# Splitting the S5 scan into four pieces and starting the next block's exchange ahead of a block's back rotation

## The chip, the cores and the metric

The kernel runs on one core of one Trainium2 chip. The core has five engines that run side by side, each through its own instructions strictly in order: TensorE (PE, matrix products and transposes), VectorE (DVE), ScalarE (ACT), GpSimd (POOL) and SyncE (SP, which here does nothing but issue DMA transfers). The metric is device microseconds (us) of one execution of the whole program.

## The reference, cut to what matters

A two-layer trunk over 1024 positions of 1024 channels. Layer 0 mixes positions with an S5 state-space mixer, layer 1 with a short gated convolution; each is followed by a SwiGLU feed-forward part and a gated per-layer embedding. The change touches the S5 mixer only:

```
def s5_mixer(u, ...):                 # u: 1024 positions x 64 groups x 16 channels
    bu = einsum('bcgk,gpk->bcgp', u, bb)      # drive of 64 complex states in each group
    h[t] = abar * h[t-1] + bu[t]              # complex diagonal recurrence over the positions
    y = real(einsum('bcgp,gkp->bcgk', h, c)) + d_skip * u
    val, gate = split(gelu(y) @ w_glu)        # the "glu" stage
    return val * sigmoid(gate)
```

## The kernel before

**Tiling.** The S5 mixer is done in eight blocks of eight groups. Positions are cut into 128 chunks of 8. Inside a chunk everything is matrix products; between the chunks a real recurrence is left, once the complex state of each chunk has been turned by a phase that makes its factor real. The 128 partitions hold the 64 real parts and the 64 imaginary parts of the states, so a complex rotation needs a copy of a tile with its two halves of 64 partitions swapped. Engines work on partitions in place, so the swap is done by two DMAs (`swapped`, L935), called the exchange here.

**A block's steps**, by the names in the code:
- `gen_in(b)` (L1127): ACT scales the input into `raw` slot r0, PE transposes it (L1138), ACT writes `U`; DVE makes two products `raw<-pwr,bbA` and `raw<-pwn,bbS` (slots r1, r2), PE adds and transposes them (L1151), ACT writes `wbt`.
- `states(b)` (L1199): PE multiplies `wbt` with `U` into the PSUM tile `pb` (L1202).
- `phases(l)` (L1106): DVE builds the phase table `ptab` of two blocks; `gen_phase(b)` (L1191) has POOL issue four DMAs that copy a block's part to `E`.
- `scan(b)` (L1205): DVE multiplies `pb` with the sines into `tmp` (two instructions, the turned part), the exchange brings `tmp` swapped to `tw`, DVE multiplies `pb` with the cosines into `sv` (the plain part), adds `tw`, runs eight scans into `gv` (L1221), and rotates back: two products into a `tmp` buffer, the P operand, and two in place in `gv`.
- `gen_out(b)` (L1155): DVE makes the output weights `W1` in three instructions, PE makes the kernel `kp` from them (L1170), ACT copies it out (L1172), POOL adds the skip term (L1176).
- `gen_swap(b)` (L1178): two DMAs write `W2`, the swapped `W1`. `gen_toeplitz(b, M)` (L1185): eight DMAs spread `kp` into the block Toeplitz matrix `M`.
- `outputs(b)` (L1229): PE, per group, `U` by `M`, P by `W1` and `gv` by `W2` (L1236 to L1238) into one PSUM bank per four groups; ACT applies GELU into `zt`.
- `channels(b, zt)` (L1243): PE transposes `zt` (L286), and the result is split in a high and a low part in `ulow` (L291 to L293), the operand of `glu`.

**Buffers.** `M`, `W2`, `sv`, `gv`, `kp`, `tw` and `zt` exist once; `W1`, `U`, `E`, `tmp` and `pb` twice. PE's short products share three PSUM banks (`tr`).

**Order.** The program text gives priorities, not the order itself: a list scheduler simulates the engines and, on each engine, issues the ready instruction that stands first in the text. The order it finds is then fixed, and every engine waits in order. `tc.issue_after(ins)` forces an instruction behind another on the same engine. Behind all the S5 work in priority stand the products of the embedding (`up_product`, L758, matmuls into `pstu`, six per tile, evacuated by ACT L770 and stored by SP L771): they fill PE's gaps, from a single PSUM bank. Their operands lie in `ulow`, whose columns `channels(4)` and later blocks overwrite, so they end before that.

**The loop** (L1258): `scan(b)`, then `gen_out(b+1)`, `outputs(b)`, `gen_phase(b+1)`, `states(b+1)`, `gen_swap(b+1)`, `gen_toeplitz(b+1)`, `gen_in(b+2)`, `channels(b)`. In the last round but one, `M` for block 7 takes a buffer of `E`, and `gen_swap(7)` comes last. After the loop `glu` loads `s5_w_glu` in pieces of 256 KB (L784), splits them into `uhigh`, whose memory belonged to the S5 tiles, and starts its products.

## Time and profile before

| | us |
|---|---|
| median of three runs | 2271.43 (2271.29 to 2271.55) |
| the profiled execution | 2275.46 |
| its span, first to last instruction | 2273.7 |
| around the span | 1.76 |
| first scan's sum starts (`sv<-sv,tw` of block 0) | 64.38 |
| last scan's sum starts (block 7) | 201.19 |
| `outputs(7)` starts | 208.21 |
| first product of `glu` | 220.45 |

Lines such as L1221 are those of the kernel before. A row of a timeline gives start, duration, engine, line, operation, written tile and read tiles, how many in one piece, and in brackets the idle time ahead of it with what ended that. SPq rows are the times that SP spent on issuing, not the transfers. A row of the table of waits gives the waiting instruction, what it waited for, the total in us, the number of times and the longest. Behind the S5 stage the diff changes only when the first weights of `glu` are asked for.

### The profile page before, as it was taken

Reading aid. Unit: us, or ns where it says so; the run is one execution under the profiler, and the core shown is the slowest. Engines: PE = TensorE matmul, PEld = TensorE weight load, DVE = VectorE, ACT = ScalarE, POOL = GpSimd, SP = SyncE. Lnnn points to the kernel's source line nnn. Section 1 sums busy time; section 2 is a strip of 40 time slices with the busy share of each in tenths; the row PEclk is TensorE's granted clock in tenths of the full one; section 3 lists DMA queues with packets and bytes.
Section 4 is the critical chain, followed back from the end, with each engine's and each line's share of the span. In section 5 each row is a group of like instructions: output and inputs, shape, how many; then the busy total and the mean of one; then the engine's idle time right before and its main releaser. Section 6 shows DMA issues by size and latency. Waiting matters only on the chain.

```text
span 2273.7 us, 27899 instructions
## 1 busy us (share of the span) xinstructions
PE 2172.8 (96%) x10001; PEld 1788.2 (79%) x10001; DVE 1646.1 (72%) x2746; ACT 910.4 (40%) x1731; POOL 359.7 (16%) x440
## 2 busy tenths in 40 slices
PE   6988999899999999999979999979999999899998
PEld 5776888688888877878868888868888888787887
DVE  7885325887777787887587776397777777788864
ACT  6554323444444443334343332154444444333342
POOL 2110001011111112342010000111111111224210
PEclk9999999899999999999989999999999999999999
DMA  7555201254444468664232334623444445876713
GB/s 247 155 130 144 91 19 60 86 169 148 158 148 157 148 227 305 249 237 166 98 107 84 93 93 146 243 93 121 160 146 157 148 156 166 330 264 222 251 64 111
DMA packets 234011, 358.14 MB, mean 158 GB/s; under 512 B 23697, under 2 KB 166033, under 8 KB 233873
## 3 DMA queue, kind: packets, MB, share of 16 engines
q1 hardware_dynamic: 203040, 247.24, 33.5%
q0 software_dynamic: 30432, 109.08, 13.6%
q8 instruction: 79, 1.29, 0.2%
q14 instruction: 60, 0.48, 0.1%
q10 hardware_dynamic: 400, 0.04, 0.0%
HBM read 225.53 MB, written 114.29 MB: 149 GB/s over the span
## 4 chain that ended last, share of the span: by engine, by line
PE 62%; issue 18%; DVE 10%; DMA 5%; POOL 3%; ACT 1%; SPq 1%; POOLq 0%; DVEq 0%; ACTq 0%
PE psmm L124 20%; PE psmm L126 20%; PE psmm L125 20%; POOL hw L485 2%; DMA w<-hw 2%; DMA tw<-tmp 1%; DVE ulow L91 1%; DVE h L627 1%; DVE gv L1221 1%; DVE W L871 1%; DVE tmp L871 1%; DVE uhigh L91 1%; PE pstr L204 1%; DVE raw L871 0%; DVE ptab L871 0%
## 5 line engine op out<-in xcount | busy, mean ns | idle before, releaser
L124 PE MATMUL psmm<-ulow,ws 128*128 128x512 f32 x896 | 354.1, 396 | 14.9 <-ACT ulow L90 9.2
L126 PE MATMUL psmm<-ulow,ws 128*128 128x512 f32 x896 | 353.0, 394 | 4.7 <-DVE ws L91 4.7
L125 PE MATMUL psmm<-ulow,ws 128*128 128x512 f32 x896 | 353.5, 395 | 0.4 <-DVE ulow L91 0.4
L126 PE MATMUL psmm<-uhigh,ws 128*128 128x512 f32 x672 | 261.6, 389 | 0.0
L125 PE MATMUL psmm<-uhigh,ws 128*128 128x512 f32 x672 | 261.5, 389 | 0.0
L124 PE MATMUL psmm<-uhigh,ws 128*128 128x512 f32 x672 | 261.5, 389 | 0.0
L90 ACT CAST ws<-raw 128x512 fp32r<-128x512 f32 x224 | 138.9, 622 | 253.7 <-PE psmm L126 248.8
L485 POOL DMA_DIRECT2D hw<-hs x154 | 116.0, 754 | 772.7 <-DVE hs L91 746.6
L124 PEld LDWEIGHTS psmm<-ulow,ws 128*128 128x128 f32 x896 | 170.9, 191 | 52.9 <-ACT ulow L90 10.8
L126 PEld LDWEIGHTS psmm<-ulow,ws 128*128 128x128 f32 x896 | 170.7, 191 | 42.4 <-DVE ws L91 6.8
L125 PEld LDWEIGHTS psmm<-ulow,ws 128*128 128x128 f32 x896 | 170.8, 191 | 37.0 <-DVE ulow L91 1.5
L627 DVE TENSOR_TENSOR h<-psmm,h 128x512 f32<-128x512 f32 x234 | 155.3, 682 | 47.9 <-PE psmm L126 29.5
L636 POOL TENSOR_TENSOR h<-part,h 128x512 f32<-128x512 f32 x100 | 139.2, 1396 | 269.9 <-ACT part L635 239.4
L124 PE MATMUL psmm<-ulow,w 128*128 128x512 f32 x380 | 152.3, 401 | 17.0 <-DVE h L627 13.4
L91 DVE TENSOR_TENSOR ws<-raw,ws 128x512 fp32r<-128x512 f32 x224 | 153.7, 688 | 13.0 <-ACT ws L90 12.9
L90 ACT CAST ws<-st 128x512 fp32r<-128x512 f32 x168 | 103.8, 619 | 130.8 <-PE psmm L126 118.9
L125 PE MATMUL psmm<-ulow,w 128*128 128x512 f32 x380 | 149.4, 393 | 0.0
L126 PE MATMUL psmm<-ulow,w 128*128 128x512 f32 x380 | 149.3, 393 | 0.0
L125 PEld LDWEIGHTS psmm<-uhigh,ws 128*128 128x128 f32 x672 | 126.2, 188 | 26.2
L124 PEld LDWEIGHTS psmm<-uhigh,ws 128*128 128x128 f32 x672 | 126.2, 188 | 26.1
L126 PEld LDWEIGHTS psmm<-uhigh,ws 128*128 128x128 f32 x672 | 126.2, 188 | 26.1
L124 PE MATMUL psmm<-w,ulow 128*128 128x512 f32 (+1 forms) x360 | 139.1, 386 | 0.0
(263 smaller groups left out, 4433.7 us busy)
## 6 DMA issues: line engine op xcount, KB each, us to landing
hw<-hs POOLq DMA_DIRECT2D x154, 512.0 KB, 4.2
w<-hw SPq DMA_DIRECT2D x88, 768.0 KB, 6.0
raw<-in_ffn_w_in_dram SPq DMA_DIRECT2D x88, 512.0 KB, 3.9
raw<-in_ffn_w_out_dram SPq DMA_DIRECT2D x44, 512.0 KB, 6.1
hd<-h POOLq DMA_DIRECT2D x24, 512.0 KB, 3.0
h<-hd SPq DMA_DIRECT2D x24, 512.0 KB, 7.3
raw<-in_conv_w_in_dram SPq DMA_DIRECT2D x24, 512.0 KB, 3.8
w<-hw SPq DMA_DIRECT2D x88, 128.0 KB, 6.1
```

Of the source, the lines that this page charges most:

```text
L90: A.copy(hi, src)
L91: V.tensor_tensor(lo, src, hi.bitcast(F32), ALU.subtract)
L124: PE.matmul(ps, ahi, bhi, start=start, stop=False, skip_group_check=more)
L125: PE.matmul(ps, ahi, blo, start=False, stop=False, skip_group_check=more)
L126: PE.matmul(ps, alo, bhi, start=False, stop=stop, skip_group_check=more)
L204: PE.transpose(pt[:, c * P:(c + 1) * P], xn[:, c * P:(c + 1) * P], ident)
L485: nc.gpsimd.dma_start(out=hidden[j][:, :, c].rearrange("q p l j -> p q l j"), in_=hs.bitcast(F32))
L627: done["sum"] = V.tensor_tensor(h[t][:, cs], ps, h[t][:, cs], ALU.add).ins
L636: G.tensor_tensor(h[t][:, cs], part, h[t][:, cs], ALU.add)
L871: V.tensor_tensor(o, a, b, op)
L1221: V.tensor_tensor_scan(gv[:, g, 1:P], dec, sv[:, g, 1:P], 0.0, ALU.mult, ALU.add)
```

## The change

`scan` is cut in four: `scan_turned` (turned part and exchange), `scan_plain`, `scan_run` (sum and scans) and `scan_back`. Round b now runs `gen_out(b+1)`, `scan_run(b)`, `scan_turned(b+1)`, `scan_back(b)`, `scan_plain(b+1)`, `outputs(b)`, `gen_toeplitz(b+1)`, `gen_swap(b+1)`, `phases`, `gen_phase(b+2)`, `gen_in(b+2)`, `states(b+2)`, `channels(b)`. `states` and `gen_phase` stand a block earlier than before. The two products of `gen_in` are forced behind the latest `scan_plain`. Block 7 gets `M` and `W2` in two halves of four groups each, in the columns of `ulow` that `channels(7)` will fill: its `gen_swap` is four DMAs, its `gen_toeplitz` sixteen, and both are issued in round 6 ahead of `scan_back(6)`. The loads of three of the four weight pieces of `glu`'s first stage are issued in round 5.

```diff
+    def glu_load(nb, u):
+        wg = s5_w_glu[0].rearrange("(kt p) (two n) -> p kt two n", p=P, two=2)
+        raw = raw_tile()
+        rv = raw.rearrange("p (kt two n) -> p kt two n", kt=2, two=2)
+        for k in range(2):
+            nc.sync.dma_start(out=rv[:, k], in_=wg[:, 2 * u + k, :, nb * 256:(nb + 1) * 256])
+        return raw
...
-                raw = raw_tile()
...
+                raw = glu_raws.pop(0) if glu_raws else glu_load(nb, u)
...
@@ -1142,7 +1148,8 @@
         shp = [P, GB, T, KG]
         Wp = [raw_tile(i).rearrange("p (g t k) -> p g t k", g=GB, t=T) for i in (1, 2)]
         for o, pw, bb in ((Wp[0], pwr, bbA), (Wp[1], pwn, bbS)):
-            tt(o, pw[:, gsl, 0:T].unsqueeze(3).broadcast_to(shp), bb[:, gsl].unsqueeze(2).broadcast_to(shp), ALU.mult)
+            with tc.issue_after(done["plain"]) if b > 1 else ExitStack():
+                tt(o, pw[:, gsl, 0:T].unsqueeze(3).broadcast_to(shp), bb[:, gsl].unsqueeze(2).broadcast_to(shp), ALU.mult)
         wbt = wbts[b] = gen.tile([P, GB, P], F32, name="wbt", tag="wbt")
         for hf in range(2):
             pt = psum(tr)
@@ -1175,18 +1182,30 @@
                         dk[:, gsl].unsqueeze(2).broadcast_to([KG, GB, KG]), ALU.mult)
         G.tensor_tensor(kp[:, :, 0, :], kp[:, :, 0, :], dd, ALU.add)
 
-    def gen_swap(b):
+    def halves(a):
+        return [a[:, hf * 4:hf * 4 + 4] for hf in range(2)]
+
+    def late_halves(q):
+        return [ulow[:, q + hf, (KT - 1) * 4 * P:KT * 4 * P].bitcast(F32).rearrange("p (g n) -> p g n", g=4) for hf in range(2)]
+
+    def gen_swap(b, parts=None):
         W1 = Ws[b]
-        W2 = W2s[b] = run.tile([P, GB, T, KG], F32, name="W2", tag="W2")
-        for a, c in ((R0, R1), (R1, R0)):
-            nc.sync.dma_start(out=W2[a].rearrange("p g s k -> p g (s k)"),
-                              in_=W1[c, :, 1:NL, :].rearrange("p g s k -> p g (s k)"))
-
-    def gen_toeplitz(b, M):
-        Ms[b], kp = M, kps[b]
-        Mv = M.rearrange("p g (t k) -> p g t k", t=T)
-        for s in range(T):
-            nc.sync.dma_start(out=Mv[s * KG:(s + 1) * KG, :, T - 1 - s:, :], in_=kp[:, :, 0:s + 1, :])
+        if parts is None:
+            parts = [run.tile([P, GB, P], F32, name="W2", tag="W2")]
+        n = GB // len(parts)
+        for i, W2 in enumerate(parts):
+            for a, c in ((R0, R1), (R1, R0)):
+                nc.sync.dma_start(out=W2[a], in_=W1[c, i * n:(i + 1) * n, 1:NL, :].rearrange("p g s k -> p g (s k)"))
+        W2s[b] = parts if len(parts) == 2 else halves(parts[0])
+
+    def gen_toeplitz(b, parts):
+        kp = kps[b]
+        n = GB // len(parts)
+        for i, part in enumerate(parts):
+            Mv = part.rearrange("p g (t k) -> p g t k", t=T)
+            for s in range(T):
+                nc.sync.dma_start(out=Mv[s * KG:(s + 1) * KG, :, T - 1 - s:, :], in_=kp[:, i * n:(i + 1) * n, 0:s + 1, :])
+        Ms[b] = parts if len(parts) == 2 else halves(parts[0])
 
     def gen_phase(b):
         E = Es[b] = run.tile([P, 2, GB, NJ], F32, name="E", tag="E", bufs=2)
@@ -1202,28 +1221,35 @@
             PE.matmul(pb[:, g * P:(g + 1) * P], wbts[b][:, g, :], Us[b][:, g, :], start=True, stop=True)
         Bs[b] = pb.rearrange("p (g j) -> p g j", g=GB)
 
-    def scan(b):
-        B = Bs[b]
-        C, S_ = Es[b][:, 0], Es[b][:, 1]
-        parts = ((slice(0, NJ - 1), slice(1, NJ), slice(NJ - 1, 0, -1), sgnN, sgnA),
-                 (slice(NJ - 1, P - 1), slice(NJ, P), slice(0, NJ), sgnA, sgnN))
+    PARTS = ((slice(0, NJ - 1), slice(1, NJ), slice(NJ - 1, 0, -1), sgnN, sgnA),
+             (slice(NJ - 1, P - 1), slice(NJ, P), slice(0, NJ), sgnA, sgnN))
+    tws = {}
+
+    def scan_turned(b):
         tm = tmp_tile()[:, 0:GB * (P - 1)]
         tv = tm.rearrange("p (g j) -> p g j", g=GB)
-        for j, _, m, _, sg in parts:
-            stt(tv[:, :, j], B[:, :, j], sg, S_[:, :, m], ALU.mult, ALU.mult)
-        tw = gen.tile([P, GB * (P - 1)], F32, name="tw", tag="tw")
-        swapped(tw, tm)
-        for j, w, m, _, _ in parts:
-            tt(sv[:, :, w], B[:, :, j], C[:, :, m], ALU.mult)
-        tt(sv[:, :, 1:P], sv[:, :, 1:P], tw.rearrange("p (g j) -> p g j", g=GB), ALU.add)
+        for j, _, m, _, sg in PARTS:
+            stt(tv[:, :, j], Bs[b][:, :, j], sg, Es[b][:, 1][:, :, m], ALU.mult, ALU.mult)
+        tws[b] = gen.tile([P, GB * (P - 1)], F32, name="tw", tag="tw")
+        swapped(tws[b], tm)
+
+    def scan_plain(b):
+        for j, w, m, _, _ in PARTS:
+            done["plain"] = V.tensor_tensor(sv[:, :, w], Bs[b][:, :, j], Es[b][:, 0][:, :, m], ALU.mult).ins
+
+    def scan_run(b):
+        tt(sv[:, :, 1:P], sv[:, :, 1:P], tws[b].rearrange("p (g j) -> p g j", g=GB), ALU.add)
         for g in range(GB):
             dec = r8[:, b * GB + g:b * GB + g + 1].broadcast_to([P, P - 1])
             V.tensor_tensor_scan(gv[:, g, 1:P], dec, sv[:, g, 1:P], 0.0, ALU.mult, ALU.add)
+
+    def scan_back(b):
+        C, S_ = Es[b][:, 0], Es[b][:, 1]
         pv = Ps[b] = tmp_tile().rearrange("p (g j) -> p g j", g=GB)
         G.memset(pv[:, :, 0:1], 0.0)
-        for _, w, m, sg, _ in parts:
+        for _, w, m, sg, _ in PARTS:
             tt(pv[:, :, w], gv[:, :, w], C[:, :, m], ALU.mult)
-        for _, w, m, sg, _ in parts:
+        for _, w, m, sg, _ in PARTS:
             stt(gv[:, :, w], gv[:, :, w], sg, S_[:, :, m], ALU.mult, ALU.mult)
 
     def outputs(b):
@@ -1233,9 +1259,9 @@
             for c in range(4):
                 g = 4 * hf + c
                 o = py[:, c * P:(c + 1) * P]
-                PE.matmul(o, Us[b][:, g, :], Ms[b][:, g, :], start=True, stop=False)
+                PE.matmul(o, Us[b][:, g, :], Ms[b][hf][:, c, :], start=True, stop=False)
                 PE.matmul(o, Ps[b][:, g, :], Ws[b][:, g, 1:NL, :], start=False, stop=False)
-                PE.matmul(o, gv[:, g, :], W2s[b][:, g], start=False, stop=True)
+                PE.matmul(o, gv[:, g, :], W2s[b][hf][:, c, :], start=False, stop=True)
             A.activation(zt[:, :, hf * 64:hf * 64 + 64].rearrange("p t (g k) -> p g t k", k=KG),
                          py.rearrange("p (g t k) -> p g t k", g=4, t=T), AF.Gelu_apprx_tanh)
         return zt
@@ -1251,37 +1277,44 @@
     phases(0)
     states(0)
     gen_phase(0)
+    scan_turned(0)
+    scan_plain(0)
     gen_out(0)
     gen_swap(0)
-    gen_toeplitz(0, M)
+    gen_toeplitz(0, [M])
     gen_in(1)
+    states(1)
+    gen_phase(1)
     for b in range(NBT):
-        scan(b)
-        nx = b + 1
+        nx, after = b + 1, b + 2
+        if nx < NBT:
+            gen_out(nx)
+        scan_run(b)
+        if nx < NBT:
+            scan_turned(nx)
+            if nx == NBT - 1:
+                late = late_halves(0)
+                for part in late:
+                    G.memset(part, 0.0)
+                gen_swap(nx, late_halves(2))
+                gen_toeplitz(nx, late)
+        scan_back(b)
+        if nx < NBT:
+            scan_plain(nx)
+        zt = outputs(b)
         if nx < NBT - 1:
-            if b % LB == 0 and b // LB + 1 < NBT // LB:
-                phases(b // LB + 1)
-            gen_out(nx)
-            zt = outputs(b)
-            gen_phase(nx)
-            states(nx)
+            gen_toeplitz(nx, [M])
             gen_swap(nx)
-            gen_toeplitz(nx, M)
-            if b + 2 < NBT:
-                gen_in(b + 2)
+        if after < NBT:
+            if after % LB == 0:
+                phases(after // LB)
+            gen_phase(after)
+            gen_in(after)
+            states(after)
+            if after == NBT - 1:
+                glu_raws.extend(glu_load(0, u) for u in range(3))
+        if nx < NBT:
             channels(b, zt)
-        elif nx < NBT:
-            states(nx)
-            gen_phase(nx)
-            gen_out(nx)
-            M = run.tile([P, GB, P], F32, name="M", tag="E", bufs=2)
-            G.memset(M, 0.0)
-            gen_toeplitz(nx, M)
-            zt = outputs(b)
-            channels(b, zt)
-            gen_swap(nx)
-        else:
-            zt = outputs(b)
     gen.release()
     mb.release()
     tu.release()
```

More of the change, by code (lines that the diff above doesn't have):

```diff
@@ L771, in up_product @@
                     nc.sync.dma_start(out=updram[l][:, t, cs], in_=ev)
+    glu_raws = []
+    def glu_load(nb, u):
[5 more added lines that the diff above has]
+        return raw
     def glu(post, ahead):
-        wg = s5_w_glu[0].rearrange("(kt p) (two n) -> p kt two n", p=P, two=2)
         rooms = [[room_high(i) for i in range(4)], [room_new(i) for i in range(4)],
@@ L780, in glu @@
             for u in range(KT // 2):
-                raw = raw_tile()
-                rv = raw.rearrange("p (kt two n) -> p kt two n", kt=2, two=2)
-                for k in range(2):
-                    nc.sync.dma_start(out=rv[:, k], in_=wg[:, 2 * u + k, :, cs])
+                raw = glu_raws.pop(0) if glu_raws else glu_load(nb, u)
                 units.append([a.rearrange("p (kt n) -> p kt n", kt=2) for a in unit_of(rooms[nb][u](), raw)])
```

## Prediction

> **What bounds the kernel now.** I read the page first, then the timeline around the S5 mixer, then the waits and the stretches inside it.
>
> ```profile
> span 2273.7 us, 27899 instructions
> ...
> PE   6988999899999999999979999979999999899998
> ...
> DVE  7885325887777787887587776397777777788864
> ```
>
> A slice is 56.8 us. PE is at 8 or 9 tenths almost everywhere, so only what shortens PE's idle stretches can win time. The change sits in slices 1 to 3, where DVE too is at 8 tenths. Its stretches, cut where the output products of blocks 0 and 5 end, and its waits:
>
> ```profile
> core 0: us, PE busy (x) PEld busy (x) DVE busy (x) ACT busy (x) POOL busy (x), PEclk, DMA share, GB/s
> 55.00:81.30 26.30, 22.98 (x157) 19.29 (x156) 20.77 (x48) 13.67 (x32) 2.23 (x6) 1.00 0.58 164
> 81.30:183.70 102.40, 93.79 (x670) 81.62 (x669) 84.58 (x166) 58.79 (x153) 19.55 (x38) 0.98 0.58 141
> ```
>
> ```profile
> DVE sv L871 <- DMA tw<-tmp: 11.3, 4, 4.6
> DVE tmp L875 <- DMA E<-ptab: 1.0, 1, 1.0
> PE pstu L124 <- ACT ev L770: 4.4, 4, 1.1
> PE pstr L1170 <- DVE W L871: 3.6, 3, 2.6
> PE pstr L286 <- ACT wbt L1153: 0.6, 1, 0.6
> ```
>
> The waits are those of 81.3 to 183.7, five rounds of 20.5 us. DVE waits there 12.3 us (11.3 + 1.0), nearly all for the exchange. PE waits 8.6 us, which is also all that its 102.4 us have beside 93.79 busy. Two engines near full, and the smaller reserve is PE's. Over the whole stage, 55 to 221, with its start and end, DVE's wait for the exchange is:
>
> ```profile
> DVE sv L871 <- DMA tw<-tmp: 23.7, 8, 5.4
> ```
>
> **What removes the exchange wait.** One block on DVE and its exchange:
>
> ```profile
> 176.84 0.75 DVE L875 SCALAR_TENSOR_TENSOR tmp<-pb,sgnN,E 128x512 f32<-128x512 f32 x1
> 177.51 1.27 DVE L871 TENSOR_TENSOR sv<-pb,E 128x504 f32<-128x504 f32 x2
> 184.14 1.22 DVE L871 TENSOR_TENSOR sv<-sv,tw 128x1016 f32<-128x1016 f32 x1 [5.36 <-DMA tw<-tmp]
> ...
> 191.37 1.28 DVE L871 TENSOR_TENSOR tmp<-gv,E 128x504 f32<-128x504 f32 x2
> 192.57 0.73 DVE L875 SCALAR_TENSOR_TENSOR gv<-gv,sgnN,E 128x504 f32<-128x504 f32 x1
> 193.22 0.74 DVE L875 SCALAR_TENSOR_TENSOR gv<-gv,sgnA,E 128x512 f32<-128x512 f32 x1
> ```
>
> The turned part ends at 177.6, the sum starts at 184.1: 6.5 us, of which the plain part covers 1.3. The change puts the back rotation (1.28 + 0.73 + 0.74 = 2.75) and the plain part behind the exchange's start, 4.0 us, and the products of the input (two, of the size of the sum, 2.4) behind those: 6.4 us against 6.5. The exchange is covered, as far as DVE goes.
>
> **What is late next.** Three rings remain, and I price each.
>
> The first is M and W2, which exist once. After the products of block 5, SP refills them:
>
> ```profile
> 183.30 0.67 SPq L1189 DMA_DIRECT2D M<-kp  x1
> 184.06 1.31 SPq L1182 DMA_DIRECT2D W<-W  x2
> 185.42 5.38 SPq L1189 DMA_DIRECT2D M<-kp  x7
> ```
>
> ```profile
> 183.29 0.39 PE L1238 MATMUL pstr<-W,gv 128*128 128x128 f32 x2
> ...
> 194.71 0.49 PE L1236 MATMUL pstr<-M,U 128*128 128x128 f32 x2
> ...
> 199.73 0.39 PE L1237 MATMUL pstr<-W,tmp 128*128 128x128 f32 x2
> 199.95 0.39 PE L1238 MATMUL pstr<-W,gv 128*128 128x128 f32 x2
> ...
> 220.45 0.74 PE L124 MATMUL psmm<-uhigh,ulow 128*128 128x512 f32 x2 [0.60 <-ACT uhigh L90]
> ```
>
> Ten issues take until 190.8, the data some 3 us more, and block 6's products run from 194.7 to 200.3. From end to end 16.7 us: no round can be shorter, but the mean round (20.5) has 3.8 us above it, 19 in five rounds. The change swaps the order (M first, then W2) at the same count, so this floor stays. SP also issues the exchange (two issues) and the stores of the embedding; an exchange asked for just after a block's products queues behind these ten issues, up to 7.5 us. It is then needed only a round later (16.7 us, of which 7.5 + 6.5 are used), so I cost that at nothing; if the cover is gone each further microsecond costs one per round.
>
> The second is DVE's own work: its waits, 12.3 us, are the most that it can give back in these rounds. E's load (POOL) moves a block ahead and stands behind the phase table; it has the scans and weights of a round to cover it, and its 1.0 us goes with the rest.
>
> The third is PE: 8.6 us of idle in the five rounds, and no matmul is removed. The embedding's products do not vanish with the gaps that they filled. Of the idle time, 3.6 is PE waiting for W. Today those three instructions come behind the sum on DVE, so they inherit the exchange wait; after the change they stand ahead of it. I take 3.6 as gone. The 4.4 are pairs of embedding tiles one behind the other, with one PSUM bank between them, which happens when PE has nothing else; with a fuller PE I take a little over half, 2.4, as gone. Together **6.0 us** in the five rounds, between 0 (every gap comes back elsewhere) and 8.6.
>
> On the first stretch, 55 to 81.3: the first exchange can't be covered by a back rotation, as there is none. DVE loses the two products of the input as cover (they are now forced behind the plain part) and gets block 1's weights and the phase table instead. PE has 3.3 us idle there. I take **1.0**, between -1 and 3.3.
>
> **The end.** From the end of block 5's products (183.7) to that of block 7's:
>
> ```profile
> 195.53 0.45 POOL L1176 TENSOR_TENSOR kp<-kp,dd 16x128 f32<-16x128 f32 x1 [0.55 <-DMA raw<-in_s_w_glu_dram]
> ```
>
> ```profile
> 197.51 6.08 SPq L1189 DMA_DIRECT2D M<-kp  x8
> 203.69 1.33 SPq L1182 DMA_DIRECT2D W<-W  x2
> ```
>
> ```profile
> 208.21 0.77 PE L1236 MATMUL pstr<-M,U 128*128 128x128 f32 x2 [4.87 <-DMA W<-W]
> ...
> 216.44 0.39 PE L1238 MATMUL pstr<-W,gv 128*128 128x128 f32 x2
> ```
>
> Before: 33.1 us (216.8 - 183.7). PE waits for W2, which SP issues last, after eight issues for M at 0.76 each, since both W2 and M's queue place wait for block 6. With rooms of its own W2 goes early. But kp exists once: block 7's kp is done 12.3 us after block 5's products (196.0 - 183.7), because block 6's M must have been read out of it first, and this doesn't change. Then sixteen issues instead of eight. No row shows a half-size one; the nearest are M's own eight, whose landing hardly goes with their size:
>
> ```profile
> M<-kp SPq DMA_DIRECT2D x8, 64.0 KB, 3.0
> ...
> M<-kp SPq DMA_DIRECT2D x8, 8.0 KB, 3.0
> ```
>
> So I price them as full ones: 16 x 0.76 = 12.2, at most, and 6.1 if half a transfer costs half. The last lands at 12.3 + 12.2 + 3.0 = 27.5, and the second half of the products (half of 5.6, by block 6) ends at 30.3, the first half being done by then. That gains 2.8; block 7's products ran at half speed at first (0.77 for a pair against 0.39) and took 8.6 instead of 5.6, so a slow second half costs 1.5 and leaves 1.3. I take **2.0**, between 1.3 and 8 (2.8 with the six-us price of the issues and a full clock). The early loads of glu:
>
> ```profile
> 191.24 1.92 SPq L784 DMA_DIRECT2D raw<-in_s_w_glu_dram  x3
> ```
>
> Six of them (0.64 each) are asked for in round 5, some of which SP made later before; they stand ahead of kp's 12.3 us and cost nothing unless M's issues slip behind them, then 3.8 at most. Behind the products nothing changes: 3.6 us to glu's first product, and from there PE is gapless, so what S5 gains reaches the end.
>
> On the slow clock: PE had 4.9 us without work ahead of 208.2, and its pairs then took twice as long. The same followed a shorter gap:
>
> ```profile
> 131.28 1.07 PE L1170 MATMUL pstr<-W,bbA 128*16 128x128 f32 x8 [2.62 <-DVE W L871]
> 132.28 0.80 PE L292 MATMUL pstr<-ulow,identn 128*128 128x512 f32 x1
> ```
>
> A single L292 there took 0.80. The gap ahead of the last products will be near 3 us, so I keep them slow. The Trainium skill (TensorE: Matmul & The Clock Gate, Part 1) has the clock halved after an idle window of about 3.4 us; by that rule the last products would run at full speed and the sum would be 1.5 us better. The 2.62 us gap with slow products behind it speaks against relying on it.
>
> **Sum.** 1.0 + 6.0 + 2.0 = 9.0 us. Profiled execution: 2275.46 - 9.0 = 2266.5; the median before is 4.03 under that execution, so **2262.4** for the median. A difference of 0.2% (4.5 us) is about what a measurement of this kernel tells from none.
>
> **Rivals.**
>
> *PE has more room than its busy time says.* Then DVE's 12.3 us come back in full, with 3.3 at the start and 2 to 3 at the end: 17 to 18 us, 2254. For: PEld is busy only 81.62 of 102.4. Against: in the stretches where the timeline shows PE back to back, pairs start every 0.22 us (199.73, 199.95) and nothing fits between them. The Trainium skill (Perfetto Trace Analysis, Identifying the Most-Contended Engine) says that matmul busy time is a bad measure of PE's headroom and that weight-load busy time is a good one, which is this rival. Chance 0.13.
>
> *The gaps move.* The waits of PE and DVE reappear at other places: DVE at the sum for an exchange that queued behind SP's refill, PE at W or ev, or the scheduler puts the turned part behind the back rotation after all, because `pb` isn't ready, so that the order hardly changes. Then 0 to 4 us remain: 2269. Against: DVE has 6.4 us of work to set behind the exchange. Chance 0.20.
>
> *Slower: DVE stands at the turned part.* It comes ahead of the back rotation now and needs the states of the next block, whose input buffer U is free only after the products of the block two before. After block 3's products (143.2) the states' second half was done late, after block 5's soon:
>
> ```profile
> 142.97 0.39 PE L1238 MATMUL pstr<-W,gv 128*128 128x128 f32 x2
> ...
> 153.14 1.05 PE L1202 MATMUL pb<-U,wbt 128*128 128x128 f32 x8
> ```
>
> ```profile
> 187.40 1.95 PE L1202 MATMUL pb<-U,wbt 128*128 128x128 f32 x16
> ```
>
> That is 11.0 and 5.7 us (189.35 - 183.68). If DVE waits in order until 11.0, a round is 11.0 + 1.5 (turned) + 2.75 (back) + 6.7 (from the back rotation's end to that of the products, 193.96 to 200.3, and some queueing) = 21.9 against 20.5: 1.4 in each of five rounds, 7 us, less 2 at the end: 2276. It decides from 9.6 us on. For: all of ACT's work on the input lies in this path. Against: a scheduler that sees pb late will run the back rotation first. Chance 0.14.
>
> **How the numbers follow.** The forecast (6 to 12 us gained) has 0.53. Faster by over 0.2%: 0.53 + 0.13 and a little of the gaps' case, 0.68; within: 0.18; slower 0.14. The forecast's own range is 2259 to 2266. The range for eight in ten reaches to the middle of the first rival (2255) and to the end of the second (2271.5).
>
> **What would show it.** Right: the wait of the sum for the exchange falls from 23.7 us in all to under 5; the five rounds between the ends of the products of blocks 0 and 5 take 96 us instead of 102.4, with PE busy 93 to 94 in them; PE's wait for W is gone; the last products wait for M, not for W2, and glu starts near 211.5. Wrong: rounds of 17 to 18 us (first rival), rounds of 20 with new waits at ev, W or the exchange (second), DVE waiting for PE L1202 (third). A stage behind S5 that gets longer or shorter by over 2 us would be wrong for all four.

## The result

The changed kernel is slower. It takes 1.0078 of the time of the kernel before (95% interval 1.0064 to 1.0092). Three runs of it, 2286.07 to 2292.24 us, are used; two others, at far lower granted clocks (0.75 and 0.30), are left out. The profiled execution went from 2275.46 to 2289.14 us, its span from 2273.7 to 2287.0. The forecast was 2262.4, so it missed by about 27 us and had the wrong sign.

All of it lies in S5. The next stage's first product starts at 234.65 us instead of 220.45, which is 14.2 later, and what follows takes as long as before to 1 us (2052.4 against 2053.3 to the end of the span). The stretches of the changed kernel, cut as before at the ends of the output products of blocks 0 and 5 and at that first product:

```profile
55.00:86.10 31.10, 27.85 (x175) 22.00 (x174) 29.18 (x63) 15.01 (x35) 6.21 (x9) 1.00 0.62 169
86.10:197.70 111.60, 95.92 (x663) 82.97 (x662) 88.22 (x164) 58.57 (x151) 21.47 (x37) 0.95 0.49 120
197.70:234.70 37.00, 26.97 (x179) 22.65 (x177) 14.21 (x25) 13.19 (x29) 1.26 (x4) 0.86 0.52 129
```

The start is 4.8 us longer (26.3 before), the five rounds 9.1 (102.4 before), the end 0.2 (36.8 before, 183.7 to 220.45). Where DVE and PE wait between 55 and 235:

```profile
DVE tmp L881 <- issue: 14.3, 3, 6.0
...
PE pstr L1264 <- DVE gv L881: 10.9, 6, 4.0
...
DVE sv L877 <- DMA tw<-tmp: 9.7, 2, 8.6
...
DVE tmp L881 <- PE pb L1221: 5.9, 1, 5.9
PE pb L1221 <- ACT wbt L1160: 5.8, 5, 2.1
...
PE pstr L1262 <- DMA ulow<-kp: 5.6, 1, 5.6
```

The wait of the sum (`sv`) for the exchange has fallen from 23.7 us in eight to 9.7 in two, and both of these lie outside the five rounds. Inside them it is gone. In its place DVE waits at the first instruction of the turned part (`tmp L881`), and PE waits for the last instruction of the back rotation (`gv L881`). One round of the changed kernel on DVE, after block 0's products ended at 86.11:

```profile
94.62 0.74 DVE L881 SCALAR_TENSOR_TENSOR tmp<-pb,sgnA,E 128x504 f32<-128x504 f32 x1 [5.92 <-PE pb L1221]
95.28 1.27 DVE L877 TENSOR_TENSOR tmp<-gv,E 128x504 f32<-128x504 f32 x2
96.48 0.74 DVE L881 SCALAR_TENSOR_TENSOR tmp<-pb,sgnN,E 128x512 f32<-128x512 f32 x1
97.14 1.27 DVE L1238 TENSOR_TENSOR sv<-pb,E 128x504 f32<-128x504 f32 x2
98.32 1.22 DVE L877 TENSOR_TENSOR raw<-pwr,bbA 128x1024 f32<-128x1024 f32 x1
99.46 1.49 DVE L877 TENSOR_TENSOR raw<-pwn,bbS 128x1024 f32<-128x1024 f32 x1
100.87 0.88 DVE L881 SCALAR_TENSOR_TENSOR gv<-gv,sgnN,E 128x504 f32<-128x504 f32 x1
101.67 0.74 DVE L881 SCALAR_TENSOR_TENSOR gv<-gv,sgnA,E 128x512 f32<-128x512 f32 x1
```

Read it as a chain. The products of block 0 free U, and `pb` of block 2 is ready 8.5 us later. Only then does DVE start the turned part, and the back rotation of block 1 (`tmp<-gv`, then the two `gv<-gv`) stands behind it, although its scans were long done. Between the two halves of the back rotation stand the plain part (1.27) and the two products of the input (2.6). It ends at 102.4, the products of block 1 at 107.4: a round of 21.3 us. In the second and fourth round the phase table runs in the wait, and a round takes 23.7, but not because of the table: the back rotation ends 16.6 and 16.2 us after the products, as in the first round (16.3). The rest is PE's. In the second round it takes the first product of `gv` 2.4 us after `gv` is ready (126.44 against 124.04), behind products of the embedding; in the fourth the products run slowly.

PE loses twice. Two of its waits for `gv` are long, and the products behind them run slowly. From the timeline of PE, and the stretches of the fourth and fifth round:

```profile
168.44 0.79 PE L1264 MATMUL pstr<-W,gv 128*128 128x128 f32 x2 [4.00 <-DVE gv L881]
...
169.45 0.63 PE L1263 MATMUL pstr<-W,tmp 128*128 128x128 f32 x2
```

```profile
152.16:175.82 23.66, 17.21 (x116) 15.14 (x115) 21.18 (x50) 10.01 (x28) 3.37 (x7) 0.86 0.36 80
175.82:197.65 21.83, 15.93 (x116) 13.86 (x115) 15.43 (x23) 9.90 (x28) 4.22 (x7) 0.92 0.39 87
```

A pair takes 0.63 instead of 0.39 us, and the granted clock is 0.86 and 0.92 there.

### The profile page after: what moved, and what is told of

Its sections match the earlier page's. It is cut to its first block, busy times and chain, and to the rows that moved or that the text cites. A ratio compares the mean times of both kernels' runs of the same rounds, so it can differ in the third digit from the quotient of the medians.

```text
span 2287.0 us, 27932 instructions
## 1 busy us (share of the span) xinstructions
PE 2181.0 (95%) x10001; PEld 1792.1 (78%) x10001; DVE 1650.6 (72%) x2746; ACT 910.8 (40%) x1731; POOL 365.2 (16%) x441
## 4 chain that ended last, share of the span: by engine, by line
PE 51%; issue 31%; DVE 6%; DMA 5%; POOL 4%; SPq 1%; ACT 1%; POOLq 0%; DVEq 0%; ACTq 0%
PE psmm L124 15%; PE psmm L125 15%; PE psmm L126 15%; POOL hw L485 4%; DMA w<-hw 1%; DMA tw<-tmp 1%; DVE ulow L91 1%; DVE h L627 1%; DMA hw<-hs 1%; PE pstr L1264 1%; PE pstr L204 1%; PE pstr L1262 0%; DVE ws L91 0%; PE pstr L1263 0%; DVE uhigh L91 0%
## 5 line engine op out<-in xcount | busy, mean ns | idle before, releaser
L124 PE MATMUL psmm<-ulow,ws 128*128 128x512 f32 x896 | 354.2, 396 | 15.7 <-ACT ulow L90 10.1
L124 PEld LDWEIGHTS psmm<-ulow,ws 128*128 128x128 f32 x896 | 170.9, 191 | 53.3 <-ACT ulow L90 11.6
L124 PE MATMUL psmm<-ulow,w 128*128 128x512 f32 x380 | 152.2, 401 | 15.1 <-DVE h L627 12.9
```

Of the source, the lines that this page charges most:

```text
L124: PE.matmul(ps, ahi, bhi, start=start, stop=False, skip_group_check=more)
```

## The experiments

Times are medians. Each run stood beside runs of the kernel before on its own chip (2271.0 to 2273.9), and the ratio is to those. The stretches are read from the profiles, cut as above: "start ends" is the end of block 0's output products, "five rounds" go from there to the end of block 5's, and "end" from there to the first product of `glu`. "Gate" stands for the `issue_after` that forces the two products of `gen_in` behind the plain part.

| run | us | ratio (95%) | start ends | five rounds | end |
|---|---|---|---|---|---|
| before | - | 1 | 81.3 | 102.4 | 36.8 |
| changed | 2289.1 | 1.0078 (1.0064-1.0092) | 86.1 | 111.5 | 37.0 |
| e1 back first | 2269.6 | 0.9980 (0.9970-0.9990) | 79.7 | 101.1 | 36.9 |
| e2 own buffer | 2270.8 | 0.9990 (0.9981-1.0000) | 78.3 | 99.1 | 39.6 |
| e3 no early loads | 2282.3 | 1.0038 (1.0023-1.0053) | 85.5 | 112.7 | 32.1 |
| e4 before, late rooms | 2272.2 | 0.9990 (0.9980-0.9999) | 83.1 | 103.4 | 34.8 |
| e5 = e1 + e3 | 2268.3 | 0.9986 (0.9977-0.9995) | 81.0 | 101.6 | 31.7 |
| e6 three buffers | 2268.9 | 0.9990 (0.9979-1.0001) | 85.6 | 98.5 | 31.0 |
| e7 weights early | 2283.0 | 1.0052 (1.0036-1.0069) | 87.3 | 105.9 | 37.0 |
| e8 no gate | 2271.1 | 0.9998 (0.9989-1.0007) | 85.3 | 98.1 | 35.4 |
| e9 gate after back | 2272.6 | 1.0000 (0.9991-1.0009) | 84.2 | 98.8 | 37.2 |
| e10 e2 + e9 + e3 | 2268.4 | 0.9991 (0.9982-1.0000) | 77.0 | 102.0 | 35.1 |
| e11 e2 + e8 + e3 | 2273.4 | 1.0007 (0.9998-1.0016) | 81.6 | 102.0 | 33.6 |
| e12 e1 + e8 + e3 | 2272.0 | 1.0000 (0.9991-1.0009) | 80.3 | 105.8 | 33.4 |
| e13 e1 in block 0 only | 2279.1 | 1.0035 (1.0023-1.0047) | 81.2 | 112.3 | 36.9 |
| e14 e13 + e9 + e3 | 2268.4 | 0.9988 (0.9979-0.9996) | 81.1 | 99.9 | 32.1 |
| e15 loads on GpSimd | 2285.4 | 1.0067 (1.0052-1.0083) | 85.6 | 112.7 | 34.3 |

Four theories stood at first. Theory 1: the two buffers of the tag `tmp` force the back rotation behind the next block's turned part, which waits for `pb`. Theory 2, its rival: the scheduler's ranking (the order of the text) does it, and the buffers have no part. Theory 3: the early loads of the next stage hold up the end. Theory 4: `pb` itself is late because of the weights. Theory 5 came from the results.

**The rounds: why the back rotation stands behind the turned part.**

```diff
         scan_run(b)
+        scan_back(b)
         if nx < NBT:
             scan_turned(nx)
...
-        scan_back(b)
```

> The changed kernel, only with the back rotation written ahead of the next block's turned part (scan_back(b) before scan_turned(nx)). Theory 1 (the two buffers of the tag tmp are handed out in the order of the text, so the back rotation stands behind the turned part, and the turned part behind a pb that comes 8.7 us after the previous outputs): the DVE waits at the turned part in front of the back rotation (5.9, 6.0, 5.3 us in the rounds 86.1 to 197.7) no longer delay outputs; the five rounds fall from 111.5 to 88-100 us (DVE alone is busy 88.2 of them), the whole to 2264-2280, start and tail as in the changed kernel. Theory 2 (the scheduler's ranking alone sets the order on DVE) expects the same of this run, since the text is its ranking. Rival (the refill of M and W2, or the products, bound the rounds at over 20): the rounds stay at 105 or more, the whole at 2283 or more.

The whole fell as expected, the rounds only to 101.1, just above the range. With the back rotation in front there is no wait at the turned part any more, but the exchange is in the open again. Between the ends of blocks 0 and 5 DVE now waits at gen_out's product, not at the sum:

```profile
DVE tmp L877 <- DMA tw<-tmp: 12.3, 6, 3.4
```

The product writes to the tag `tmp`, whose buffer the exchange still reads. So the two buffers of this tag bind three uses: the turned part, gen_out's product and P.

```diff
-        return run.tile([P, GB * P], F32, name="tmp", tag="tmp", bufs=2)
+        return run.tile([P, GB * P], F32, name="tmp", tag="tmp")
+
+    def turn_tile():
+        return run.tile([P, GB * P], F32, name="tmq", tag="tmq")
...
     def scan_turned(b):
-        tm = tmp_tile()[:, 0:GB * (P - 1)]
+        tm = turn_tile()[:, 0:GB * (P - 1)]
```

> The changed kernel with its text in the same order, but the ring of two buffers tmp divided: one for gen_out's product and the back rotation's P, one (tmq) for the turned part, so no more memory. Theory 1 (the shared ring holds the back rotation back): the back rotation is issued ahead of the turned part, the five rounds fall to 88-100 us as in the run with the back rotation first, the whole to 2264-2280. Theory 2 (the order comes from the ranking alone, and the ring has no part in it): 2286-2292, as the changed kernel, with DVE waits of 3 to 6 us at the turned part in front of the back rotation.

Theory 2 falls: with the same text and the same amount of memory, the order on DVE turns round. Of the run with the divided ring:

```profile
107.82 1.28 DVE L877 TENSOR_TENSOR tmp<-gv,E 128x504 f32<-128x504 f32 x2
...
109.83 0.75 DVE L881 SCALAR_TENSOR_TENSOR gv<-gv,sgnA,E 128x512 f32<-128x512 f32 x1
...
110.70 0.74 DVE L881 SCALAR_TENSOR_TENSOR tmq<-pb,sgnA,E 128x504 f32<-128x504 f32 x1
```

The rounds (99.1) and the whole came out as expected of theory 1; the end grew by 2.6 us, which was not followed up. The buffers of a ring go out in the order of the text. With one ring, P of block b comes behind the turned part of block b+1, whatever the ranking would prefer.

**The rounds: what the order costs.** The next run was meant to let ready work into the waits.

```diff
         for o, pw, bb in ((Wp[0], pwr, bbA), (Wp[1], pwn, bbS)):
-            with tc.issue_after(done["plain"]) if b > 1 else ExitStack():
+            if True:
```

> The changed kernel without the order by hand that holds gen_in's two weight products on DVE until the next block's plain part. Theory: the gate keeps 2.7 us of ready work out of the DVE's waits at the turned part (5.9, 6.0, 5.3 us); without it the products fill them and the weights are ready earlier, five rounds 103-109, the whole 2280-2288. Rival (the scheduler puts them where they delay the back rotation in the rounds that have the phase table): 2289-2296.

It gained 18 us where 1 to 9 were expected, and that with the back rotation still behind the turned part. So theory 1 was not the whole, and I formed theory 5: a round is one chain, and what counts is how much DVE does between `pb` and the end of the back rotation. The run that tells this from filling the waits holds the two products of the input back further still, to the end of the back rotation, so that nothing fills the waits:

```diff
-            done["plain"] = V.tensor_tensor(sv[:, :, w], Bs[b][:, :, j], Es[b][:, 0][:, :, m], ALU.mult).ins
+            tt(sv[:, :, w], Bs[b][:, :, j], Es[b][:, 0][:, :, m], ALU.mult)
...
-            stt(gv[:, :, w], gv[:, :, w], sg, S_[:, :, m], ALU.mult, ALU.mult)
+            done["plain"] = V.scalar_tensor_tensor(gv[:, :, w], gv[:, :, w], sg, S_[:, :, m], ALU.mult, ALU.mult).ins
```

> The changed kernel, its two weight products of gen_in held until the end of the back rotation instead of the end of the plain part. In the changed kernel they run (2.6 us) between the plain part and the second half of the back rotation. Theory 5 (the round is one chain: outputs' end, 8.5 us to the turned part, then all that DVE does up to the back rotation's end, then the last products; so every instruction between the turned part and the back rotation's end counts once a round, and none of the rest): the five rounds fall by 5 x 2.4 to 98-101 us, as without the gate (98.1), the whole from about 2290 to 2273-2279, with the DVE waits of 5 to 6 us at the turned part still there. Rival (without the gate it was the filling of those waits, or earlier weights, that gained): with the waits still there, the rounds stay at 108 or more and the whole at 2284 or more.

DVE's waits inside its five rounds, the same place on DVE's timeline, and its fourth round:

```profile
DVE tmp L881 <- issue: 11.8, 3, 5.3
```

```profile
95.22 1.26 DVE L877 TENSOR_TENSOR sv<-pb,E 128x504 f32<-128x504 f32 x2
96.40 0.73 DVE L1253 SCALAR_TENSOR_TENSOR gv<-gv,sgnN,E 128x504 f32<-128x504 f32 x1
97.05 0.74 DVE L1253 SCALAR_TENSOR_TENSOR gv<-gv,sgnA,E 128x512 f32<-128x512 f32 x1
97.72 1.21 DVE L877 TENSOR_TENSOR raw<-pwr,bbA 128x1024 f32<-128x1024 f32 x1
```

```profile
145.09:164.93 19.84, 18.16 (x134) 15.75 (x134) 18.95 (x45) 11.72 (x31) 4.90 (x10) 1.00 0.60 151
```

The waits are still there and the rounds take 98.8, which is 12.7 less. The two products, 2.6 us, now come behind the back rotation, and this ends 13.2 to 15.1 us after the last block's products instead of 15.6 to 16.6. Round by round the gain is 1.5, 2.4, 1.3, 3.8 and 3.8 us, so it is not simply the 2.6 us in each. In the first and the third round PE takes the first product of `gv` only 1.6 us after `gv` is ready, behind other products that it had before it. In the last two rounds the long waits of PE and the slow clock went as well: the granted clock is 1.00 in the fourth round where it was 0.86. Why the scheduler had put the gated products ahead of the second half of the back rotation, no run shows.

The loss took the ring and the gate together. The ring alone, without the gate (e8) or with the gate elsewhere (e9), costs the rounds nothing against before: 98.1 and 98.8 against 102.4. Nor does the gate alone, with the ring divided (e2): 99.1.

The chain's other end is `pb`. Here the part of gen_in from `xg` to `U` moves behind the copy into `wbt`:

```diff
-        xg = raw_tile(0).rearrange("p (g t k) -> p g t k", g=GB, t=T)
...
-        U = Us[b] = run.tile([P, GB, P], F32, name="U", tag="U", bufs=2)
...
             A.copy(wbt[:, 4 * hf:4 * hf + 4].rearrange("p c n -> p (c n)"), pt)
+        xg = raw_tile(0).rearrange("p (g t k) -> p g t k", g=GB, t=T)
...
+        U = Us[b] = run.tile([P, GB, P], F32, name="U", tag="U", bufs=2)
...
```

> The changed kernel with its order of back rotation and turned part, but in gen_in the weights' transposes and copy (wbt) are written ahead of the scaled input and its transposes, so that pb waits for the input alone. Theory 4 (the turned part waits because pb comes 8.7 us after the previous outputs, held by the weights' transposes and their copy): pb comes 1.5 to 3 us earlier, the five rounds fall from 111.5 to 100-106 us, the whole to 2276-2287. Rival (the input's part, behind the U buffer that outputs sets free, is the whole of the chain): pb no earlier, 2288-2293.

The turned part of the first round starts 7.3 us after the products (94.53 - 87.26) instead of 8.5, and the rounds are 5.6 shorter: 1.2 x 5 is 6.0. That is a sum over rounds of 17.4 to 25.3 us, as DVE's order shifted as well, so it agrees with the chain but does not isolate it.

**The end: the early loads.**

```diff
-            if after == NBT - 1:
-                glu_raws.extend(glu_load(0, u) for u in range(3))
```

> The changed kernel without the three weight loads of the next stage issued ahead (they are issued where the next stage begins, as before). Theory 3 (six load issues of 4.4 us stand on SP ahead of the last block's exchange, and their 1.5 MB lengthen its landing from 4.2 to 7.5 us): the last sum's wait of 8.6 us falls to 2.5-4, the stretch from outputs(5)'s end to the next stage's first product from 37.0 to 31-34, the whole to 2283-2287. Rival (M's sixteen issues of the last block bound the tail: PE waits 5.6 for M now): the sum comes earlier, M does not, and the whole is within 2 us of the changed kernel.

SP's queue in the changed kernel, and the sum on DVE that it holds up:

```profile
204.35 4.40 SPq L780 DMA_DIRECT2D raw<-in_s_w_glu_dram  x6
208.86 1.19 SPq L943 DMA_DIRECT2D tw<-tmp  x2
210.09 4.10 SPq L1198 DMA_DIRECT2D ulow<-W  x4
214.30 10.94 SPq L1207 DMA_DIRECT2D ulow<-kp  x16
```

```profile
217.04 1.22 DVE L877 TENSOR_TENSOR sv<-sv,tw 128x1016 f32<-128x1016 f32 x1 [8.62 <-DMA tw<-tmp]
```

The turned part of block 7 ended at 205.8, but the exchange was issued at 208.86. Without the early loads:

```profile
207.52 1.21 SPq L943 DMA_DIRECT2D tw<-tmp  x2
208.77 0.79 SPq L1198 DMA_DIRECT2D ulow<-W  x1
209.66 11.52 SPq L1207 DMA_DIRECT2D ulow<-kp  x16
```

The sum's wait falls to 3.9 us, M starts 4.6 earlier, and the end takes 32.1 instead of 37.0. The rival (M bounds the end whatever the loads do) falls: M's own issues had slipped too, though PE still waits 2.2 us for M. To part the place on SP from the bytes, the same loads went out by GpSimd:

```diff
-            nc.sync.dma_start(out=rv[:, k], in_=wg[:, 2 * u + k, :, nb * 256:(nb + 1) * 256])
+            (nc.gpsimd if nb == 0 and u < 3 else nc.sync).dma_start(out=rv[:, k], in_=wg[:, 2 * u + k, :, nb * 256:(nb + 1) * 256])
```

> The changed kernel with its early loads of the next stage's weights issued by GpSimd instead of SP, so that they move the same bytes at about the same time but stand ahead of nothing on SP. Theory 3a (the place on SP costs, 4.4 us of issues ahead of the exchange and of M's sixteen loads): the end stretch falls from 37.0 to 33-34.5, the whole to 2284-2288. Theory 3b (the 1.5 MB in flight cost, the exchange lands in 7.3 us instead of 4.5): the stretch stays at 36 or more, the whole at 2287-2292. If neither by itself: under 33, as without the loads (32.1).

The end takes 34.3, in the range of theory 3a: 2.7 of the 4.9 us were the place on SP, where M's sixteen issues start 13.9 us after block 5's products instead of 16.7. The other 2.2 go with the bytes, but this run does not part them cleanly. GpSimd issued the loads from 199.0 on, 5 us before SP did, so they met block 6's refill too: its W2 took 9.1 us to land instead of 4.1, and PE waited 3.0 us for it. The exchange, from issue to landing in the end stretch, takes 7.3 us in the changed kernel, 4.5 without the loads, and 8.4 with the loads on GpSimd, where the sum still waits 8.4 us for it:

```profile
W<-W SPq DMA_DIRECT2D x2, 256.0 KB, 9.1
...
tw<-tmp SPq DMA_DIRECT2D x2, 254.0 KB, 8.4
```

The rooms alone, in the kernel before (the Toeplitz matrix and the exchanged weights of block 7 in halves of `ulow`, loaded ahead of `outputs(6)`), with the changed kernel's `late_halves`, `gen_swap` and `gen_toeplitz`:

```diff
-            M = run.tile([P, GB, P], F32, name="M", tag="E", bufs=2)
-            G.memset(M, 0.0)
-            gen_toeplitz(nx, M)
+            late = late_halves(0)
+            for part in late:
+                G.memset(part, 0.0)
+            gen_swap(nx, late_halves(2))
+            gen_toeplitz(nx, late)
             zt = outputs(b)
             channels(b, zt)
-            gen_swap(nx)
```

> The kernel before with one part of the change alone: the last block's Toeplitz matrix and exchanged weights in the free rooms of ulow, in two halves each, loaded ahead of outputs(6). Before, the last products wait 4.9 us for the exchanged weights (issued on SP at 203.7, behind M). Theory (the rooms let those weights in early): that wait goes, what is late next is M with 16 issues in place of 8, about 6 us more of SP, so 0 to 3 us gained: 2268-2272. Rival (the sixteen issues put off the last exchange or the loads of the next stage on SP): 2273-2278.

The end is 2.0 shorter. PE's wait for the exchanged weights (4.9) is gone, and a wait for M has come (`ulow<-kp`, 4.1). Start and rounds were 1.8 and 1.0 longer in this profile, for which I have no reason to give. The whole is 0.1% faster, at the edge of what can be told.

**The start.**

```diff
         scan_run(b)
+        if b == 0:
+            scan_back(b)
         if nx < NBT:
             scan_turned(nx)
...
-        scan_back(b)
+        if b > 0:
+            scan_back(b)
```

> The changed kernel with the back rotation written ahead of the turned part for block 0 alone. Theory 5 for the start (there too the back rotation stands behind the turned part, with the phase table run in the wait): outputs(0) ends at 78-81 instead of 86.1, the rounds after it stay at 110-113, the end at 36-38: the whole 4 to 7 under the changed kernel, 2281-2286. Rival (the start's 4.8 us come from the earlier products and tables of the next block, whatever the order): outputs(0) ends at 84 or later, the whole at 2287 or more.

In the changed kernel the scans of block 0 end at 68.2, the back rotation follows at 74.40 behind the turned part:

```profile
65.64 2.61 DVE L1244 TENSOR_TENSOR_SCAN gv<-r,sv 128x127 f32<-128x127 f32 x8
...
73.75 0.74 DVE L881 SCALAR_TENSOR_TENSOR tmp<-pb,sgnA,E 128x504 f32<-128x504 f32 x1
74.40 1.48 DVE L877 TENSOR_TENSOR tmp<-gv,E 128x504 f32<-128x504 f32 x2
```

With block 0's back rotation first it starts at 67.97, and `outputs(0)` ends at 81.2, 4.9 earlier. The rival falls: the work brought forward is the same. The whole, 2279.1, fell by more than the 4.2 us that its next stage starts earlier; the rest lies behind S5 (below).

**Do the terms add?** Six runs put cures together, with the edits shown above.

> Both effects found so far together: the back rotation written first, and no early loads of the next stage's weights. If they add (theory 1 for the rounds, theory 3 for the end): the end stretch falls from 36.9 us (outputs(5)'s end to the next stage's first product, with the back rotation first) to 31-33, the whole to 2264-2267 where the back rotation first alone gave 2269.6. Rival (with the exchange early, the sixteen loads of M bound the end): the last sum's wait falls but the stretch stays over 35.5, the whole at 2268-2271.

The end went from 36.9 to 31.7, as theory 3 has it. The whole does not show it: it is 0.14% under before where the back rotation first alone gave 0.20%, and lies in the range of the rival, whose reason does not hold.

Then to the own buffer, the back rotation first and no loads, this:

```diff
-        tm = tmp_tile()[:, 0:GB * P].rearrange("p (g s k) -> p g s k", g=GB, s=T)
+        tm = raw_tile(0).rearrange("p (g s k) -> p g s k", g=GB, s=T)
```

> As the last, and no sharing is left: the turned part and the back rotation's P have a buffer each, and gen_out's product goes into the room of gen_in's scaled copy, so no memory is added. With the back rotation first, the DVE still waits 12.3 us in the rounds, at gen_out's product, whose shared buffer the exchange still reads. Theory 1 extended (the shared buffer is what keeps the exchange from being covered): those waits go to under 4, the five rounds fall from 101.1 to 92-97 us (DVE busy 87), the whole to 2256-2263. Rival (behind the exchange the phase table on DVE, or the products with 92 us busy, bound the rounds): the waits go, the rounds stay at 99-102, the whole at 2263-2267.

Neither side came out. The rounds (98.5) and the whole (2268.9) stay above the theory's ranges, and the waits did not go: DVE waits 11.5 us for the exchange in the five rounds (20.3 over the whole stage), now at the sum, since gen_out's product no longer stands in front of it and the phase table still comes behind it. Rounds without a phase table take 17.7 us, those with one 22.

> All that helped, together: own buffer for the turned part, the two weight products behind the back rotation, no early loads. If the terms add: start at outputs(0)'s end 78-81 (own buffer: 78.3), five rounds 96-100, end stretch 31-33 to the next stage's first product at 206-213: 2257-2265. Rival (the rounds are bound at 99 to 101 by the exchange, with the phase table on DVE in half of them): 2264-2269.

The start was the shortest of all, 77.0, but the rounds took 102.0, with 22.3 us of DVE waiting for the exchange over the stage. The whole is in the rival's range, and the rounds are a little above its 99 to 101.

> Own buffer for the turned part, no gate, no early loads. If what counts is that nothing stands between the scans and the back rotation's end, this equals the last to 3 us: 2257-2268. Rival: the phase table, which is spread over the scans in this order, delays the back rotation by up to 4 us in three rounds: 2266-2275.

The whole lies in the rival's range, with rounds of 102.0; where in them the phase table costs was not followed up.

> The back rotation written first, no gate, no early loads. By the chain of theory 5 the gate has no part where the back rotation comes first: the same as with the gate (2268.3) to 3 us, 2265-2271. Rival (the gate costs by itself): 2255-2264.

A microsecond above the range. Dropping the gate gains nothing where the back rotation comes first, as theory 5 has it; that its rounds are 4.2 longer than with the gate is not explained by it.

> The three terms undone, each in the way that left the most: block 0's back rotation first (start), the two weight products behind the back rotation (rounds), no early loads (end). If the terms add: outputs(0) ends at 78-81, five rounds 98-100, end stretch 31-33: next stage's first product at 207-213, the whole 2257-2264. Rival (what is gained at the start is lost again in the first rounds, which wait for the refill of M and W2 or for the exchange): 2265-2271.

The stretches of the last one:

```profile
55.00:81.10 26.10, 24.17 (x163) 19.81 (x162) 23.45 (x51) 13.62 (x32) 3.69 (x5) 1.00 0.59 157
81.10:181.00 99.90, 93.84 (x679) 81.42 (x677) 87.81 (x167) 59.88 (x154) 26.60 (x41) 1.00 0.59 147
181.00:213.08 32.08, 24.59 (x180) 21.15 (x177) 16.40 (x32) 13.19 (x29) 1.26 (x4) 0.95 0.58 150
```

In S5 the terms add in this run, where in e10 and e12 the rounds did not. Against the changed kernel the start gives 5.0, the rounds 11.6, the end 4.9; the next stage starts at 213.08, 21.6 earlier, and 7.4 earlier than before. The whole is 2268.4, which is what its rival expected, though not for the rival's reason: only 2.6 us (0.12%, interval 0.04 to 0.21) of the 7.4 are left. The two profiled executions do differ by 7.5 (2275.46 and 2267.94). But that of before was itself 4.0 above its median, so its start of the next stage may be late for its kind; no run here shows where those 4 us lay. The e1, e5 and e14 versions beat the kernel before by 0.1 to 0.2%.

## Why the prediction was wrong

**The step that failed** is the cover of the exchange: "6.4 us against 6.5. The exchange is covered, as far as DVE goes." The sum was right and its place was wrong. The back rotation and the products of the input were taken as work that fills the time behind the exchange's issue. But the next products wait for the back rotation, and the products of the input ran ahead of its second half. The step counted what DVE has to do, not what stands in line between `pb` and the end of the back rotation. What is put there as cover, the plain part and the products of the input, 3.9 us a round, delays the end of the back rotation. e9 took the larger part, 2.6 us, out again, and the five rounds fell by 12.7, between 1.3 and 3.8 each.

**The third rival named the mechanism and its chance was too low** (0.14), for the reason given against it: "a scheduler that sees pb late will run the back rotation first." It could not. P and the turned part share a ring handed out in the order of the text (e2). The rival's price came out for another sum than it gave. It had `pb` at 11.0 us; `pb` came at 8.5, under its own threshold of 9.6, and its sum with 8.5 gives 19.5, which is what e8 and e9 measure (19.6 and 19.8). That agreement is partly luck: the sum leaves out the plain part (1.3 us), and its last leg of 6.7 us, from the back rotation's end to that of the products, is 6.2 in e9's first round. The rest, to 22.3, is the gated products, PE's other products ahead of those of `gv`, and the slow clock, none of which it had.

**The three rings.** The floor of the refill was put at 16.7 us. From block 5 to 6 the changed kernel takes 15.6 (197.65 to 213.21), so it is no floor. It was not what bound either: none of the five rounds came under 17.4 in any run. PE's wait for W is gone, as forecast. PE's busy time was forecast at 93 to 94 and is 95.92, and its idle time 15.7 us where it was 8.6 before. With the gated products out of the way the rounds take 98.8 where 96.4 was forecast, so the 6.0 us were mis-sized by 2.4 and not wrong in sign: 3.6 came.

**The start** was forecast 1.0 shorter and came 4.8 longer; the working looked at the cover of the first exchange and not at the back rotation of block 0, which is held by the same ring (e13: 4.9).

**The end** was forecast 2.0 shorter. The rooms gave that in the kernel before (e4: 2.0), and without the early loads the changed kernel gets 4.7 (32.1 against 36.8). The last products wait for M and no longer for W2, as forecast, and sixteen issues took 10.94 us, between the 6.1 and 12.2 that were the bounds. The failed part is that the early loads "cost nothing unless M's issues slip behind them, then 3.8 at most": the exchange of block 7 slipped behind them, then M behind the exchange, and the bytes slowed its landing. Together 4.9.

**Behind S5** nothing was to change by over 2 us. For the changed kernel that holds (0.9). Among the experiments this part varied from 2047 to 2055 us with its text unchanged, so single profiles can't be compared in the whole to better than some 8 us. Stretches inside S5 can, to about 2 us: that is how far they moved where an edit did not touch them (1.8 in e4's start, 1.2 in the rounds of e3).

## What to carry to other kernels

When a step is moved to cover a transfer, follow the buffer it writes to as well as the data: two uses that share a ring of buffers are issued in the order of the text, however late the first one's input is. Work that covers one wait is only free if nothing later waits for the last instruction of it, so put cover behind the instruction that frees the next engine, not in front of it. A load for the next stage that is issued early takes its place in the queue and its share of the transfers from whatever is urgent there; issue it behind the last urgent transfer.

## What the runs showed of the hardware

A wait of PE costs more than its length. Behind gaps of 4.00 and 3.46 us (blocks 4 and 5 of the changed kernel), pairs of 128x128 products took 0.63 in place of 0.39 us for 5.6 and 3.1 us, and a gap of 5.56 ahead of the last products did the same for about 7. In e9's five rounds, with waits for `gv` of 1.1 us at most and no gap above 2.10, the granted clock stayed at 1.00. The Trainium skill (TensorE: Matmul & The Clock Gate, Part 1) has the clock halved behind an idle window of about 3.4 us; the three long gaps agree with it. Below that, the length of the gap alone does not decide. Gaps of 2.62 us (the prediction's) and 1.82 (e6, at 115.63) were followed by slow products as well, gaps of 2.92 (e12, at 131.76) and 2.68 (e6, at 205.42) were not, and no run here shows what made the difference.

The landing of a small exchange depends on what else is in flight more than I had thought: the same two transfers of 254 KB took 4.5 us without the early weight loads (six of 256 KB) and 7.3 to 8.4 with them.
